# A 16-row write from SBUF to the output as SyncE's first transfer, in an RMSNorm-SiLU kernel

## The chip, the cores and the metric

The kernel runs on one core of a Trainium2 chip. A core has a matrix engine (TensorE, PE in the profile), a vector engine (VectorE, DVE), a scalar engine (ScalarE, ACT), GpSimd (POOL) and SyncE (SP), which here only issues transfers. Transfers between the memory of the chip (HBM) and the core's own memory (SBUF, 128 partitions) run on 16 DMA engines that all issuing queues share. The metric is the device time of one execution in microseconds; smaller is better.

## The reference

```python
def reference(x, gamma, eps):                 # x: 8 x 1024 x 2048 f32, gamma: 2048 f32
    rms = np.sqrt(np.mean(x ** 2, axis=-1, keepdims=True) + eps)
    out = gamma * x / rms
    return (out * (1 / (1 + np.exp(-out)))).astype(np.float32)
```

Each of the 8192 rows of 2048 numbers is divided by its root mean square, multiplied by gamma, and put through SiLU. 67.1 MB are read and 67.1 MB are written.

## The kernel before

The 8192 rows are cut into 16 blocks of 512 rows. A block lies on the 128 partitions with four rows (J = 4) on each, so a block is 4.19 MB and a partition's share of it is one contiguous run of 32 KB in HBM (blocks 4 and 5 are loaded together, with 64 KB for each partition). A ring in SBUF, `xt` (line 57), holds six blocks (BUFS = 6); a block is loaded into its place in the ring, changed in place and stored from there, so block b + 6 can be loaded only when block b has been stored.

For each block the steps are:

- `load` (line 68; line 72 for the pair of blocks 4 and 5), issued from ScalarE's queue;
- the sum of squares of each row, two of four rows on ScalarE (`squares_scalar`, line 89) and two on VectorE (`squares_vector`, line 98);
- the root on ScalarE (`root`, line 108) and its reciprocal on VectorE (`invert`, line 114);
- the product of row, reciprocal and gamma on VectorE (`multiply`, line 124);
- SiLU on ScalarE, two rows at a time (`silu`, line 129);
- `store` (line 133), issued from SyncE's queue. SyncE issues nothing else but one transfer of gamma at the start.

The order of all this is written out by hand (`tc.manual_schedule()`, line 135); every engine runs its instructions in that order and waits on semaphores where it needs another's result. Blocks 0 and 1 are done singly, the others in pairs that share one root and one reciprocal.

At the start, gamma has to be brought to all 128 partitions. SyncE loads it into the first partition of the tile `g` (line 141). TensorE multiplies it with one partition of the tile `ones` (line 144; `ones` is 128 x 128 and is filled by VectorE in line 138), VectorE copies the result from PSUM to `g` (line 146), and a one-element copy on ScalarE (line 147) waits for that. Behind this copy on ScalarE stand the loads of blocks 2 to 5; the loads of blocks 0 and 1 stand ahead of it.

```python
load(0)
nc.vector.memset(ones, 1.0)
nc.vector.memset(eps_t, float(eps))
nc.scalar.activation(out=junk_a[:, 0:1], in_=ones[:, 0:1], func=ACT.Square)
nc.sync.dma_start(out=g[0:1, :], in_=bass.AP(tensor=gamma.tensor, offset=gamma.offset, ap=[[d, 1], [1, d]]))
```

Of the kernel before, what the change touches and what calls it, by code (L numbers as in the profile page):

```python
# [1 line left out]

# [4 lines left out]

ACT = mybir.ActivationFunctionType
ALU = mybir.AluOpType


@with_exitstack
def kernel(
    ctx: ExitStack,
    tc: tile.TileContext,
    x: bass.AP,
    gamma: bass.AP,
    eps: bass.AP,
    out: bass.AP,
):  # L20

    nc = tc.nc
    P = nc.NUM_PARTITIONS
    f32 = mybir.dt.float32
    x2 = x.flatten_outer_dims()
    o2 = out.flatten_outer_dims()  # L30
    n, d = x2.shape
    J = 4
    BUFS = 6
    SINGLE = 2
    nblk = n // (P * J)
    PAIRS = (4,)

    def view(t, b):

        for q in PAIRS:  # L40
            if b in (q, q + 1):
                both = t[q * P * J:(q + 2) * P * J, :].rearrange("(p j) d -> p (j d)", p=P, j=2 * J)
                return both[:, (b - q) * J * d:(b - q + 1) * J * d]
        return t[b * P * J:(b + 1) * P * J, :].rearrange("(p j) d -> p (j d)", p=P, j=J)

    singles = ctx.enter_context(tc.tile_pool(name="singles", bufs=1))
    small = ctx.enter_context(tc.tile_pool(name="small", bufs=2))
    psum = ctx.enter_context(tc.tile_pool(name="psum", bufs=1, space=bass.MemoryType.PSUM))

    Q = 4  # L50
    w = d // Q
    g = singles.tile([P, d], f32)
    eps_t = singles.tile([P, 1], f32)
    ones = singles.tile([P, P], f32)
    junk_a = psum.tile([P, d], f32, name="junk_a")
    junk_v = psum.tile([P, d], f32, name="junk_v")
    ring = singles.tile([P, BUFS * J * d], f32, name="xt")
    sss, rmss, rstds = {}, {}, {}

    def rows(b, j, k):  # L60
        at = (b % BUFS) * J + j
        return ring[:, at * d:(at + k) * d]

    def row(b, j):
        return rows(b, j, 1)

    def load(b):
        nc.scalar.dma_start(out=rows(b, 0, J), in_=view(x2, b))  # L68

    def load_pair(b):  # L70
        both = x2[b * P * J:(b + 2) * P * J, :].rearrange("(p j) d -> p (j d)", p=P, j=2 * J)
        nc.scalar.dma_start(out=rows(b, 0, 2 * J), in_=both)

    def group(b):

        return [b] if b < SINGLE else [b, b + 1]

    def sums(b):
        if b not in sss:
            k = len(group(b))  # L80
            t = small.tile([P, k * J], f32, name="ss")
            for i, m in enumerate(group(b)):
                sss[m] = (t, i * J)
        return sss[b]

    def squares_scalar(b, loads=()):
        t, at = sums(b)
        for j in range(share(b)):
            nc.scalar.activation(out=junk_a, in_=row(b, j), func=ACT.Square,  # L89
                                 accum_out=t[:, at + j:at + j + 1])  # L90
            if j == 0:
                for s in loads:
                    load(s)

    def squares_vector(b):
        t, at = sums(b)
        for j in range(share(b), J):
            nc.vector.tensor_tensor_reduce(  # L98
                out=junk_v, in0=row(b, j), in1=row(b, j), scale=1.0, scalar=0.0,
                op0=ALU.mult, op1=ALU.add, accum_out=t[:, at + j:at + j + 1])  # L100

    def share(b):
        return 2

    def root(b):
        k = len(group(b)) * J
        rms = small.tile([P, k], f32, name="rms")
        nc.scalar.activation(out=rms, in_=sss[b][0], func=ACT.Sqrt, scale=1.0 / d, bias=eps_t)  # L108
        rmss[b] = rms

    def invert(b):
        k = len(group(b)) * J
        rstd = small.tile([P, k], f32, name="rstd")
        nc.vector.reciprocal(out=rstd, in_=rmss.pop(b))  # L114
        for i, m in enumerate(group(b)):
            rstds[m] = (rstd, i * J)

    def scale(b, j):
        t, at = rstds[b]
        return t[:, at + j:at + j + 1]  # L120

    def multiply(b):
        for j in range(J):
            nc.vector.scalar_tensor_tensor(out=row(b, j), in0=row(b, j), scalar=scale(b, j),  # L124
                                           in1=g, op0=ALU.mult, op1=ALU.mult)

    def silu(b):
        for h in range(0, J, 2):
            nc.scalar.activation(out=rows(b, h, 2), in_=rows(b, h, 2), func=ACT.Silu)  # L129
        store(b)  # L130

    def store(b):
        nc.sync.dma_start(out=view(o2, b), in_=rows(b, 0, J))

    with tc.manual_schedule():

        load(0)
        nc.vector.memset(ones, 1.0)  # L138
        nc.vector.memset(eps_t, float(eps))  # L139
        nc.scalar.activation(out=junk_a[:, 0:1], in_=ones[:, 0:1], func=ACT.Square)  # L140
        nc.sync.dma_start(out=g[0:1, :], in_=bass.AP(tensor=gamma.tensor, offset=gamma.offset, ap=[[d, 1], [1, d]]))
        for c in range(Q):
            cols = slice(c * w, (c + 1) * w)
            nc.tensor.matmul(junk_v[:, cols], ones[0:1, :], g[0:1, cols], start=True, stop=True)  # L144
        load(1)
        nc.vector.tensor_copy(out=g, in_=junk_v)  # L146
        nc.scalar.copy(out=junk_a[:, 0:1], in_=junk_v[:, d - 1:d])  # L147
        for b in range(2, PAIRS[0]):
            load(b)
        for b in PAIRS:  # L150
            load_pair(b)


        squares_scalar(0)
        squares_vector(0)
        root(0)
        invert(0)
        multiply(0)
        squares_scalar(1)
        silu(0)  # L160
        squares_vector(1)
        root(1)
        invert(1)
        multiply(1)
        squares_scalar(2)
        silu(1)
        squares_vector(2)

        for b in range(SINGLE, nblk, 2):
            squares_scalar(b + 1, [b + 3] if BUFS <= b + 1 and b + 3 < nblk else [])
            squares_vector(b + 1)
            root(b)
            invert(b)
            multiply(b)
            multiply(b + 1)
            silu(b)
            ahead = b + 2
            if ahead < nblk:  # L180
                if b == SINGLE:
                    load(BUFS)
                    silu(b + 1)
                    squares_scalar(ahead, [BUFS + 1])
                    squares_vector(ahead)
                    continue
                squares_scalar(ahead, [ahead + 2] if ahead + 2 < nblk else [])
                squares_vector(ahead)
            silu(b + 1)


# [1 line left out]
_INS = ['x', 'gamma', 'eps']  # L193
_OUTS = [((8, 1024, 2048), 'float32')]

_NUMBERS = {'eps': 9.999999747378752e-06}


# [26 lines left out]
```

## Time and profile before

| | |
|---|---|
| time, median of 3 runs | 316.79 us (316.77 to 316.83) |
| time of the profiled execution | 316.85 us |
| span of the profiled execution | 315.1 us |
| moved | 134.24 MB, 426 GB/s over the span |
| VectorE busy | 224.6 us (71%) |
| ScalarE busy | 204.6 us (65%) |
| TensorE busy | 7.2 us (2%) |
| DMA's share of the chain that ended last | 51% |
| a store, from issue to landing (median) | 41.0 us |
| a load, from issue to landing (median) | 25.4 us |

The span runs from the first to the last instruction that the profiler saw; the rest of the execution's time, 1.75 us, lies around it. In the profile q10 is the queue of the loads (ScalarE's) and q1 that of gamma and of the stores (SyncE's). "SPq" and "ACTq" are the issuing parts of SyncE and ScalarE. In the timeline a line has the start, the length, the engine, the line of the kernel, the operation, and in brackets how long the engine had been idle and what ended it; instructions of one kind that lie close together are merged, with their count behind an x.

### The profile page before, as it was taken

What the parts mean: (1) busy time and instruction counts of PE and PEld (TensorE: products, weight loads), DVE (VectorE), ACT (ScalarE), POOL (GpSimd) and SP (SyncE); (2) the same over time, 40 slices, a digit from 0 to 9 for tenths busy, and PEclk for the clock granted to TensorE, in tenths of its full rate; (3) what the DMA queues carried; (4) which work ended last, traced back from release to release, by engine and by line L of the source; (5) the groups of instructions that cost most, each with busy time, mean ns of one, the idle gap of its engine ahead of it and who ended that gap; (6) DMA issues with size and microseconds to landing.
All of it is one profiled execution on the core that took longest, in us unless ns stands there. A gap on an engine that the chain in (4) does not pass through costs nothing.

```text
span 315.1 us, 402 instructions
## 1 busy us (share of the span) xinstructions
PE 7.2 (2%) x8; PEld 2.5 (1%) x8; DVE 224.6 (71%) x140; ACT 204.6 (65%) x126; POOL 0.2 (0%) x4
## 2 busy tenths in 40 slices
PE   6200000000000000000000000000000000000000
PEld 2000000000000000000000000000000000000000
DVE  0679599799806998299923999149991599979500
ACT  1259998488365896658916689066890679957800
POOL 0000000000000000000000000000000000000000
DMA  8999999999999999999999999999999999999996
GB/s 334 412 453 412 387 528 399 399 408 458 405 458 409 453 412 453 416 449 416 449 416 449 420 445 424 441 424 441 433 433 437 433 433 433 433 433 433 437 437 300
DMA packets 4468, 134.24 MB, mean 426 GB/s; under 512 B 497, under 2 KB 497, under 8 KB 497
## 3 DMA queue, kind: packets, MB, share of 16 engines
q10 hardware_dynamic: 2160, 67.11, 49.8%
q1 hardware_dynamic: 2306, 67.12, 49.4%
q14 instruction: 2, 0.02, 0.0%
HBM read 67.12 MB, written 67.11 MB: 426 GB/s over the span
## 4 chain that ended last, share of the span: by engine, by line
DMA 51%; DVE 22%; ACT 18%; issue 3%; DVEq 1%; ACTq 0%
DMA out_dram<-xt 44%; DVE xt L124 20%; ACT xt L129 10%; DMA xt<-in_x_dram 7%; ACT junk_a L89 5%; DVE junk_v L98 2%; ACT L108 2%; DVEq L220 1%; ACT rms L108 0%; ACTq L68 0%; ACT L129 0%; DVE rstd L114 0%; DVE ss L98 0%; ACT L140 0%; ACTq L108 0%
## 5 line engine op out<-in xcount | busy, mean ns | idle before, releaser
L124 DVE SCALAR_TENSOR_TENSOR xt<-xt,rstd,g 128x2048 f32<-128x2048 f32 x64 | 145.6, 2345 | 0.3
L129 ACT ACTIVATE xt<-xt 128x4096 f32<-128x4096 f32 x32 | 115.0, 3611 | 35.9 <-DVE xt L124 35.9
L89 ACT ACTIVATE junk_a<-xt 128x2048 f32<-128x2048 f32 x32 | 59.9, 1873 | 45.8 <-DMA out_dram<-xt 41.2
L98 DVE CUSTOM_DVE_ANT_0 junk_v<-xt 128x2048 f32<-128x2048 f32 x32 | 73.5, 2298 | 1.5 <-DMA xt<-in_x_dram 0.7
L114 DVE RECIPROCAL rstd<-rms 128x8 f32<-128x8 f32 (+1 forms) x9 | 1.8, 198 | 59.8 <-ACT rms L108 59.8
L108 ACT ACT_TABLE_LOAD x9 | 11.5, 1283 | 2.1 <-DVE ss L98 1.9
L129 ACT ACT_TABLE_LOAD x9 | 11.5, 1283 | 0.2
L146 DVE COPY g<-junk_v 128x2048 f32<-128x2048 f32 x1 | 2.3, 2291 | 9.1 <-PE junk_v L144 9.1
L144 PE MATMUL junk_v<-g,ones 1*128 1x512 f32 x8 | 7.2, 1072 | 2.9 <-DMA g<-in_gamma_dram 2.9
L147 ACT COPY junk_a<-junk_v 128x1 f32<-128x1 f32 x1 | 0.1, 144 | 9.9 <-DVE g L146 9.9
L89 ACT ACTIVATION_READ_ACCUMULATOR junk_a<-xt 128x1 f32 x32 | 6.0, 186 | 0.0
L98 DVE DVE_READ_ACCUMULATOR2_ANT ss<- 128x1 f32 x32 | 4.5, 140 | 0.0
L108 ACT ACTIVATE rms<-ss,eps_t 128x8 f32<-128x8 f32 (+1 forms) x9 | 2.7, 300 | 0.1
L144 PEld LDWEIGHTS junk_v<-g,ones 1*128 1x128 f32 x8 | 2.5, 325 | 6.0 <-issue 6.0
L140 ACT ACT_TABLE_LOAD x1 | 1.3, 1283 | 1.1 <-PEq L206 1.1
L138 DVE MEMSET ones<- 128x128 f32 x1 | 0.2, 165 | 0.8 <-PEq L206 0.8
L140 ACT ACTIVATE junk_a<-ones 128x1 f32<-128x1 f32 x1 | 0.2, 174 | 0.0
L206 POOL MEMSET const-bfloat16-1.0<- 128x1 bf16 x1 | 0.1, 102 | 0.0
L206 POOL MEMSET const-uint8-127<- 128x1 uint8 x1 | 0.1, 102 | 0.0
L206 POOL MEMSET const-float32-0.0<- 128x1 f32 x1 | 0.1, 99 | 0.2 <-issue 0.2
L206 POOL MEMSET const-float32-1.0<- 128x1 f32 x1 | 0.1, 99 | 0.0
L139 DVE MEMSET eps_t<- 128x1 f32 x1 | 0.1, 59 | 0.0
## 6 DMA issues: line engine op xcount, KB each, us to landing
out_dram<-xt SPq DMA_DIRECT2D x16, 4096.0 KB, 41.0
xt<-in_x_dram ACTq DMA_DIRECT2D x14, 4096.0 KB, 25.4
g<-in_gamma_dram SPq DMA_DIRECT2D x1, 8.0 KB
xt<-in_x_dram ACTq DMA_DIRECT2D x1, 62.0
```

The lines of the kernel that those rows point to most:

```text
L89: nc.scalar.activation(out=junk_a, in_=row(b, j), func=ACT.Square, accum_out=t[:, at + j:at + j + 1])
L98: nc.vector.tensor_tensor_reduce(out=junk_v, in0=row(b, j), in1=row(b, j), scale=1.0, scalar=0.0, op0=ALU.mult, op1=ALU.add, accum_out=t[: ...
L108: nc.scalar.activation(out=rms, in_=sss[b][0], func=ACT.Sqrt, scale=1.0 / d, bias=eps_t)
L114: nc.vector.reciprocal(out=rstd, in_=rmss.pop(b))
L124: nc.vector.scalar_tensor_tensor(out=row(b, j), in0=row(b, j), scalar=scale(b, j), in1=g, op0=ALU.mult, op1=ALU.mult)
L129: nc.scalar.activation(out=rows(b, h, 2), in_=rows(b, h, 2), func=ACT.Silu)
L138: nc.vector.memset(ones, 1.0)
L140: nc.scalar.activation(out=junk_a[:, 0:1], in_=ones[:, 0:1], func=ACT.Square)
L144: nc.tensor.matmul(junk_v[:, cols], ones[0:1, :], g[0:1, cols], start=True, stop=True)
L146: nc.vector.tensor_copy(out=g, in_=junk_v)
L206: nc = _bacc.Bacc("TRN2", target_bir_lowering=False, num_devices=1)
L220: with _tile.TileContext(nc) as tc:
```

## The change

A new function, `first_words_out`, is called between ScalarE's first activation and the load of gamma. It issues one transfer from SyncE. Its source is the tile `ones`: the first 128 numbers (512 bytes) of every eighth partition, sixteen rows in all. Its destination is the place of block 15 in the output: the first 512 bytes of every eighth partition's run of 32 KB, so the sixteen pieces lie 256 KB apart. The last store of the kernel writes the whole of block 15 later, over these pieces.

```diff
     def store(b):
         nc.sync.dma_start(out=view(o2, b), in_=rows(b, 0, J))
 
+    def first_words_out():
+
+        w0, G = 128, 16
+        last = view(o2, nblk - 1).rearrange("(a c) f -> a c f", a=G)
+        nc.sync.dma_start(out=last[:, 0, 0:w0], in_=ones.rearrange("(a c) f -> a c f", a=G)[:, 0, 0:w0])
+
     with tc.manual_schedule():
 
         load(0)
         nc.vector.memset(ones, 1.0)
         nc.vector.memset(eps_t, float(eps))
         nc.scalar.activation(out=junk_a[:, 0:1], in_=ones[:, 0:1], func=ACT.Square)
+        first_words_out()
         nc.sync.dma_start(out=g[0:1, :], in_=bass.AP(tensor=gamma.tensor, offset=gamma.offset, ap=[[d, 1], [1, d]]))
```

The order of the instructions on TensorE, VectorE, ScalarE and GpSimd stays as it was; SyncE has one transfer more, ahead of gamma's. The transfers take their semaphores from eight in turn, so from gamma on each has the next one of the eight; load 6 waits for store 0, as before, and now also for the new transfer, whose semaphore it takes over.

## The prediction

> **What bounds the kernel now.** I read the page first, for the DMA rows. Columns of the two slice rows: forty slices of 7.9 us; the first row is the mean busy share of the 16 DMA engines in tenths, the second what they moved.
>
> ```profile
> span 315.1 us, 402 instructions
> DMA  8999999999999999999999999999999999999996
> GB/s 334 412 453 412 387 528 399 399 408 458 405 458 409 453 412 453 416 449 416 449 416 449 420 445 424 441 424 441 433 433 437 433 433 433 433 433 433 437 437 300
> DMA packets 4468, 134.24 MB, mean 426 GB/s; under 512 B 497, under 2 KB 497, under 8 KB 497
> q10 hardware_dynamic: 2160, 67.11, 49.8%
> q1 hardware_dynamic: 2306, 67.12, 49.4%
> ```
>
> The transfers never rest: all slices but the first and last are at nine tenths or more, and the rate without mixing (late slices) is 433 GB/s, 27.06 GB/s for one of 16 engines. 134.24 MB at 433 take 310.0 us of the span of 315.1. VectorE (71%) and ScalarE (65%) have room. So only two things can change the time: packet time that carries no bytes, and a moment with nothing queued.
>
> For the first I set the DMA share of some stretches beside the bytes of the same stretches (columns: stretch, length, busy of five engines with counts, clock, DMA share, GB/s).
>
> ```profile
> 1.00:4.00 3.00, 1.09 (x2) 0.60 (x3) 0.00 (x0) 1.46 (x2) 0.00 (x0) 1.00 0.96 319
> 4.00:20.00 16.00, 6.07 (x8) 1.89 (x6) 7.38 (x7) 5.73 (x7) 0.00 (x0) 1.00 1.00 432
> 36.00:40.00 4.00, 0.00 (x0) 0.00 (x0) 3.18 (x3) 3.96 (x5) 0.00 (x0) 1.00 1.10 385
> 40.00:52.00 12.00, 0.00 (x0) 0.00 (x0) 11.93 (x8) 11.38 (x8) 0.00 (x0) 1.00 1.01 437
> 52.00:68.00 16.00, 0.00 (x0) 0.00 (x0) 14.23 (x10) 9.50 (x7) 0.00 (x0) 1.00 1.06 459
> ```
>
> A share of 1.00 goes with 432 to 433 GB/s: in 4 to 20, in 40 to 52 (437 by 1.01) and in 52 to 68 (459 by 1.06). Two stretches break this. In 36 to 40 the engines are booked 1.10 x 4 = 4.40 us each, and the bytes need 385/432.5 x 4 = 3.56: on the mean engine 0.84 us of packet time without bytes. In 1 to 4 it is 2.88 against 2.21: 0.67 us. The second is load 0, the first reads of x. What is the first?
>
> ```profile
> 0.72 0.38 ACTq L68 DMA_DIRECT2D xt<-in_x_dram  x1
> 0.73 0.33 SPq L141 DMA_DIRECT2D g<-in_gamma_dram  x1
> 0.82 0.17 DVE L138 MEMSET ones<- 128x128 f32 x1 [0.82 <-PEq L206]
> 2.91 7.16 PE L144 MATMUL junk_v<-g,ones 1*128 1x512 f32 x8 [2.91 <-DMA g<-in_gamma_dram]
> 12.51 0.82 ACTq L68 DMA_DIRECT2D xt<-in_x_dram  x2
> 22.67 1.88 ACT L89 ACTIVATE junk_a<-xt 128x2048 f32<-128x2048 f32 x1 [3.11 <-DMA xt<-in_x_dram]
> 28.86 2.29 DVE L98 CUSTOM_DVE_ANT_0 junk_v<-xt 128x2048 f32<-128x2048 f32 x1
> 35.17 35.51 SPq L133 DMA_DIRECT2D out_dram<-xt  x3
> ```
>
> The timeline has one event ahead of it: SyncE issues the first store at 35.17, the first transfer of the kernel from SBUF to HBM. Later stores begin without such a loss. The single packet records, strung by their times into the 16 engines, say the same finer: every engine loses 0.47 to 1.59 us on the load packets between 36 and 40, mean 0.84, and the engine that ends last in the whole kernel is the one that lost 1.59. Taking from each engine its own loss brings the last end forward by 0.82 us (the next engines lost 0.75 and 0.90).
>
> **The change, part by part.** It removes nothing and adds one transfer, which I call the touch: from SBUF to the output, sixteen rows of 512 B, on SyncE ahead of gamma. No engine's compute instructions change, and loads and stores keep their order.
>
> *The touch's bytes.* One row for each engine, if it is split as loads are: 512/27,060 = 0.02 us, and a count for the semaphore. The packet price has no row of its own. Bounds: nothing below; above, the whole time in which engines are booked or waiting beyond the bytes, 315.1 - 310.0 = 5.1 us, less the two losses (1.5), shared over 497/16 = 31 small packets an engine: 0.12 us each, 0.23 for two. The small-packet row bounds it loosely, since start and end of the span are in it; I take 0.08.
>
> *The touch's wait.* It reads the tile of ones, so it waits for the memset, 0.82 + 0.17 = 0.99. Behind it on SyncE is gamma alone, which went out at 0.73 and now follows at about 1.0 + 0.41 (two loads took 0.82) = 1.4: 0.7 late. On its DMA engine gamma also meets load 0, which it used to precede: up to one load packet more (32 KB at 27.06 GB/s = 1.21), and up to another around the touch. So gamma comes 0.7 to 3.1 late, and I take 1.9.
>
> The Trainium skill, DMA: Bandwidth & Descriptors, section "Queues, rings and completion order", says that a DMA engine takes turns between the queues it has work for, one packet at a time. By that rule gamma's delay would be the 1.9, not the 0.7.
>
> *Who waits for gamma.* The matmuls (7.16), the copy of g, ScalarE's copy at 12.49, behind which loads 2 to 5 stand, then block 0's work. Loads 0 and 1 keep the DMA engines busy to 22.65, and a load takes about 1 us from issue to its first packet (0.72 to the 1 to 2 us stretch), so loads 2 to 5 may be some 9 us late. Block 0: ScalarE ends root 0 at 19.56 and waits 3.11 until 22.67 for block 1; the second silu starts near 31.6 and its rows are done at 28.86, 2.7 earlier; VectorE's squares of block 1 end at 33.6 and ScalarE wants them at 35.16, 1.5 later. A delay of 1.9 costs store 0 nothing and root 1 about 0.4; and at 36 the DMA engines still have 24 MB less 34 us x 433 GB/s = 10 MB of loads queued, 23 us of work. It costs nothing. Were that cover gone, it would cost up to 3.1.
>
> *New waits later.* The queues' semaphores move on by one place: load 6 also waits for the touch, and the last store lies over bytes that the touch wrote. Load 6 is issued at 67.41, some 60 us after the touch. The tail holds too: the last store, issued at 299.7, lands 13.9 later, where its 4.19 MB need 9.7 and its start 1, so about 3 us of older stores cover any lateness.
>
> *The first-store loss.* If it belongs to the first write from SBUF to the output, whichever it is, the touch takes it, at about 2 to 3 us instead of 36 to 40. There load 0's own empty 0.67 us runs. Not shown by the trace: how much of the touch's stall lies under it. Bounds: all of it (the end comes 0.82 sooner, 0.08 for the touch: -0.74) and none (0.84 paid at the start: about +0.10). That gamma's engine ran gamma before load 0 and still lost time at store 0 says that the loss is not a matter of SyncE's queue being new. I take the full cover as likeliest: gamma's first read and load 0's first reads were in flight together, and gamma landed (matmul at 2.91) before load 0's empty time was over, so first accesses overlap there. Sum: 315.1 - 0.82 + 0.08 = 314.4 span; the profiled execution took 316.85 with 1.75 around its span, and the median is 316.79, so **316.05**, 0.23% faster. 0.2% (0.63 us) is about what a measurement of this kernel can tell from no change.
>
> **Rivals.**
> *The loss is moved, not hidden.* The touch stalls load 0's packets at the start as store 0 stalls load packets now. For it: at store 0 the packets that lost time are loads, on another queue. Against: load 0 is waiting anyway. Time 316.79 + 0.08 - up to 0.4 of partial cover: 316.4 to 316.9, middle 316.7.
> The Trainium skill, DMA: Bandwidth & Descriptors, section "Back-pressure in remote DMA", states that stalled writes hold up the other queues of the same engine. It speaks of transfers between cores; by it this rival would hold and the time would be 316.7. The trace agrees that loads are held when store 0 begins; whether they would be at 2 us no run shows yet.
>
> *The loss belongs to a queue that starts beside a running one.* After the touch the queue is empty until 35.17, so store 0 loses its 0.84 again, and the touch adds its packets: 316.85. For it: the queue of stores is never empty again until the end, so no restart shows it free. In this case the change has no hold on the loss at all.
>
> *Slower: both are paid.* The loss belongs to the part of the output that is first written. The touch writes in block 15's place, 15 x 4.19 = 63 MB behind block 0's; it stalls all engines at the start (0.84) and store 0 stalls them again. 316.79 + 0.84 + 0.08 = 317.7. It decides if stores 0 to 15 each had such a loss; against it, the stretches after 40 us show none, though each store goes to a new 4 MB.
>
> **Chances and range.** Hidden at least in the main 0.50, moved 0.20, restart 0.14, both paid 0.16. The first's own range is 315.7 (some engines' lateness gone too) to 316.3, with 0.42 of its 0.50 beyond 0.63 us. Faster 0.42; same 0.08 + 0.20 + 0.14 = 0.42; slower 0.16. The range for 8 in 10 leaves out most of the last: 315.75 to 317.1.
>
> **What would show it.** DMA share and bytes of the stretch 36 to 40 should agree again (1.00 by 432); if 1.10 by 385 stays, the restart or the both-paid case holds. In 1 to 4 the difference should stay near 0.67; if it grows to 1.5, the loss was moved. Gamma's matmul should begin at 3.6 to 6 instead of 2.91, store 0 be issued at 35.2 to 35.7, and the last landing come 0.7 sooner. I am wrong if an idle DMA stretch appears anywhere after 4 us, or if the last store is issued over 3 us later against the bytes left.

## The result, and the profile after

The changed kernel took 319.40 us (median of four, 319.28 to 320.12), the kernel before 316.81 in the same comparison: a ratio of 1.0087, 95% interval 1.0075 to 1.0098. The change costs 2.6 us. Forecast were 316.05 and a range of 315.75 to 317.1.

The rows of the page that answer to those shown of the kernel before (the profiled execution took 320.12 us, the longest of the four, so what follows explains 3.2 us and not 2.6):

```profile
span 318.3 us, 404 instructions
DMA  8999999999999999999999999999999999999995
GB/s 330 409 449 432 424 395 453 420 399 399 432 409 417 445 441 420 445 416 441 428 441 445 416 445 424 432 436 432 449 412 445 424 436 436 432 441 420 441 424 235
DMA packets 4500, 134.25 MB, mean 422 GB/s; under 512 B 513, under 2 KB 529, under 8 KB 529
```

The transfers still never rest. There are 32 packets more: sixteen of the touch and sixteen counts of its semaphore. So the time has gone where no row of tenths shows it. The timeline of the changed kernel:

```profile
0.72 0.37 ACTq L68 DMA_DIRECT2D xt<-in_x_dram  x1
1.02 0.58 SPq L139 DMA_DIRECT2D out_dram<-ones  x1
1.66 0.45 SPq L148 DMA_DIRECT2D g<-in_gamma_dram  x1
10.61 7.16 PE L151 MATMUL junk_v<-g,ones 1*128 1x512 f32 x8 [10.61 <-DMA g<-in_gamma_dram]
20.21 0.82 ACTq L68 DMA_DIRECT2D xt<-in_x_dram  x2
40.32 16.05 SPq L133 DMA_DIRECT2D out_dram<-xt  x2
72.99 0.33 ACTq L68 DMA_DIRECT2D xt<-in_x_dram  x1
76.57 0.33 SPq L133 DMA_DIRECT2D out_dram<-xt  x1
```

Gamma goes out 0.93 us later than before (1.66 against 0.73) and lands 7.7 us later: its matmul starts at 10.61, not 2.91. The loads of blocks 2 to 5 follow at 20.21 (12.51 before), store 0 at 40.32 (35.17), load 6 at 72.99. In the kernel before load 6 went out 5.6 us earlier:

```profile
67.41 0.34 ACTq L68 DMA_DIRECT2D xt<-in_x_dram  x1
```

The stretches, read as in the prediction (DMA share times length, less the time that the bytes need at 432.5 GB/s):

```profile
1.00:4.00 3.00, 0.00 (x0) 0.00 (x0) 0.00 (x0) 1.46 (x2) 0.00 (x0) 1.00 0.99 317
36.00:40.00 4.00, 0.00 (x0) 0.00 (x0) 3.97 (x4) 3.44 (x2) 0.00 (x0) 1.00 0.91 393
40.00:52.00 12.00, 0.00 (x0) 0.00 (x0) 10.26 (x7) 10.68 (x9) 0.00 (x0) 1.00 1.04 410
52.00:68.00 16.00, 0.00 (x0) 0.00 (x0) 14.15 (x12) 10.38 (x8) 0.00 (x0) 1.00 1.01 432
68.00:100.00 32.00, 0.00 (x0) 0.00 (x0) 25.61 (x17) 25.23 (x15) 0.00 (x0) 1.00 1.00 414
100.00:200.00 100.00, 0.00 (x0) 0.00 (x0) 79.55 (x49) 70.07 (x40) 0.00 (x0) 1.00 1.00 432
```

The loss of 36 to 40 us has only moved with store 0: it is now in 40 to 52 (12.48 - 11.38 = 1.10 us on the mean engine), and 52 to 68 has 0.18. New is 68 to 100: 32.00 - 30.63 = 1.37 us of packet time without bytes, where the kernel before had none (30.40 - 30.41):

```profile
68.00:100.00 32.00, 0.00 (x0) 0.00 (x0) 19.79 (x15) 20.32 (x14) 0.00 (x0) 1.00 0.95 411
```

In all 2.65 against 0.84, so 1.8 us more on the mean engine. In 1 to 4 us little changed: 2.97 - 2.20 = 0.77, against 0.67. The packet records, strung into the 16 engines as in the prediction, give the rest: the engines end 1.83 us later on average, and the last of them 2.0 us behind the mean instead of 0.6. 1.83 + 1.40 = 3.2, the difference of the spans, 318.3 - 315.1.

The packet records also tell why gamma is so late. Times in us from the start of the span, rounded; the touch's and gamma's packets are on SyncE's queue:

```
                          before            changed kernel
first load packets        1.7 to 2.5        1.7 to 2.3
touch, 16 packets         -                 6.1 to 6.6
touch, 16 counts          -                 7.3 to 7.9
gamma's packet            1.7               8.6
gamma's count             2.5              10.1
```

On every engine three load packets run ahead of the touch. Then each packet of SyncE's queue waits for one load packet of 1.21 us, and a four-byte count is a packet too: touch, load, count, load, gamma, load, count.

### The profile page after: what moved, and what is told of

The parts are those of the page before. It is cut to its first block, busy times and chain, and to the rows that moved or that the text cites. A ratio compares the mean times of both kernels' runs of the same rounds, so it can differ in the third digit from the quotient of the medians.

```text
span 318.3 us, 404 instructions
## 1 busy us (share of the span) xinstructions
PE 7.2 (2%) x8; PEld 2.5 (1%) x8; DVE 224.6 (71%) x140; ACT 205.0 (64%) x126; POOL 0.2 (0%) x4
## 4 chain that ended last, share of the span: by engine, by line
DMA 54%; DVE 26%; ACT 10%; PE 2%; issue 2%; DVEq 1%; ACTq 1%; SPq 0%
DMA out_dram<-xt 42%; DVE xt L124 19%; DMA xt<-in_x_dram 9%; ACT xt L129 6%; DVE junk_v L98 5%; DMA g<-in_gamma_dram 3%; PE junk_v L151 2%; ACT L108 2%; ACT junk_a L89 2%; DVE g L153 1%; DVEq L227 1%; ACT rms L108 0%; ACTq L68 0%; DVE rstd L114 0%; DVE ss L98 0%
```

## Experiments

Two theories stood at first. *Late gamma*: the touch costs only because gamma lands late, and with it block 0's work. *The touch itself*: sixteen rows on the store queue, or an early write to the output, make later transfers dearer.

**The touch behind gamma.**

```diff
-        first_words_out()
         nc.sync.dma_start(out=g[0:1, :], in_=...)
+        first_words_out()
```

> Gamma's load and the touch change places on SyncE; both stay. Theory of the late gamma (the touch costs only because gamma now lands at 10.6 us instead of 2.9, and store 0 goes out at 40.3 instead of 35.2): gamma's matmul near 2.9 us, store 0 near 35.2, time 316.5 to 317.1. Theory of the touch itself (sixteen rows on the store queue make the later stores dearer, whenever gamma comes): 318.5 to 319.5 with matmul near 2.9. If besides the touch takes over the loss of the first store, the stretch 36 to 40 agrees with its bytes and the time is 316.0.

Measured: 316.83 us against 316.71, ratio 0.9998 (0.9989 to 1.0007). Lines of its timeline and three of its stretches:

```profile
1.14 0.56 SPq L139 DMA_DIRECT2D out_dram<-ones  x1
2.57 7.16 PE L151 MATMUL junk_v<-g,ones 1*128 1x512 f32 x8 [2.57 <-DMA g<-in_gamma_dram]
35.24 0.37 SPq L133 DMA_DIRECT2D out_dram<-xt  x1
```

```profile
1.00:4.00 3.00, 1.43 (x2) 0.83 (x3) 0.00 (x0) 1.46 (x2) 0.00 (x0) 1.00 0.93 319
36.00:40.00 4.00, 0.00 (x0) 0.00 (x0) 3.11 (x3) 3.96 (x5) 0.00 (x0) 1.00 1.07 352
68.00:100.00 32.00, 0.00 (x0) 0.00 (x0) 19.39 (x14) 20.38 (x14) 0.00 (x0) 1.00 0.96 414
```

The same touch is there, and the whole cost is gone; 68 to 100 loses 30.72 - 30.63 = 0.1 us. The theory of the touch itself falls. And the first-store loss is still there: 4.28 - 3.26 = 1.02 us in 36 to 40 (0.84 before), while 1 to 4 loses 2.79 - 2.21 = 0.58 (0.67 before). The touch takes over nothing.

**Gamma late without a touch.** Gamma's transfer waits for two clearings of its row by VectorE:

```diff
+        for _ in range(2):
+            nc.vector.memset(g[0:1, :], 0.0)
         nc.sync.dma_start(out=g[0:1, :], in_=...)
```

> No touch; gamma's transfer waits for two clearings of its own row by VectorE and so lands several us late. Late gamma: matmul at 7 to 11 us, store 0 at 37 to 41 us, time 318 to 319.5. Touch itself: 316.8.

Measured: 320.93 us (320.57 to 321.65), ratio 1.0130 (1.0112 to 1.0147). It was later than meant, hence above the 319.5:

```profile
5.40 0.33 SPq L143 DMA_DIRECT2D g<-in_gamma_dram  x1
11.83 2.04 PE L146 MATMUL junk_v<-g,ones 1*128 1x512 f32 x2 [11.83 <-DMA g<-in_gamma_dram]
41.54 0.36 SPq L133 DMA_DIRECT2D out_dram<-xt  x1
```

Late gamma alone slows the kernel. Issued at 5.40, it still takes 6.4 us to its matmul, with nothing of SyncE's ahead of it. Here loads 2 to 5, issued at 21.43, also came too late: by the packet records the mean engine stands idle for 0.7 us before 30 us, against none in the kernel before. That is likely why this run costs more than the changed kernel.

**A read in the touch's place**, of the same shape, from x into a spare tile:

```diff
-        last = view(o2, nblk - 1)...
-        nc.sync.dma_start(out=last[:, 0, 0:w0], in_=ones...)
+        last = view(x2, nblk - 1)...
+        nc.sync.dma_start(out=spare...[:, 0, 0:w0], in_=last[:, 0, 0:w0])
```

> The touch is replaced by a transfer of the same shape and place in the queue that reads sixteen 512-byte rows of x into a spare tile; nothing is written to the output ahead of store 0. Late gamma: as the changed kernel, matmul near 10.6 and 319.2 to 319.6. A cost of writing the output early: under 318.

Measured: 319.70 us, ratio 1.0085 (1.0071 to 1.0100), matmul at 10.58. VectorE clears the spare tile first (not shown in the cut of the edit), so the read goes out at 1.16, the touch at 1.02. Whether the sixteen rows are written to the output or read from x makes no difference that these runs show.

**Loads 2 to 5 ahead of the copy that waits for gamma**, in the changed kernel:

```diff
+        for b in range(2, PAIRS[0]): load(b)
+        for b in PAIRS: load_pair(b)
         nc.vector.tensor_copy(out=g, in_=junk_v)
         nc.scalar.copy(out=junk_a[:, 0:1], in_=junk_v[:, d - 1:d])
-        for b in range(2, PAIRS[0]): load(b)
-        for b in PAIRS: load_pair(b)
```

> The changed kernel, with the loads of blocks 2 to 5 issued ahead of ScalarE's copy that waits for gamma. Gamma stays late. If the lateness of these loads costs, about 317; if the lateness of block 0's work and of store 0 costs, 319 to 319.6, with store 0 still after 39 us.

Measured: 319.09 us, ratio 1.0073 (1.0058 to 1.0089), store 0 at 40.03. The lateness of these loads is at most 0.3 of the 2.6 us; block 0's late work carries the rest.

**Gamma behind a small clearing, no touch.**

```diff
+        nc.vector.memset(g[0:1, 0:128], 0.0)
         nc.sync.dma_start(out=g[0:1, :], in_=...)
```

> No touch; gamma's transfer waits only for a small clearing by VectorE, so it goes out at about 1.2 us, 0.5 later than before but behind load 0. If being behind load 0's packets is the larger part of gamma's delay (three load packets of 1.21 us ahead, one more before its count): matmul at 7.5 to 8.5 us, store 0 near 37.5 to 39. Time: half of the late gamma's cost, 317.3 to 318.8. If gamma is only 0.5 late: matmul near 3.5 and 316.8.

Measured: 317.81 us, ratio 1.0038 (1.0017 to 1.0060); the ten runs lie in two groups of five, 316.8 to 317.2 and 318.4 to 319.4, and the median lies between them. The profiled run, 318.43, is of the upper group.

```profile
1.15 0.33 SPq L142 DMA_DIRECT2D g<-in_gamma_dram  x1
8.30 5.45 PE L145 MATMUL junk_v<-g,ones 1*128 1x512 f32 x6 [8.30 <-DMA g<-in_gamma_dram]
38.01 0.37 SPq L133 DMA_DIRECT2D out_dram<-xt  x1
```

```profile
68.00:100.00 32.00, 0.00 (x0) 0.00 (x0) 23.60 (x17) 23.32 (x15) 0.00 (x0) 1.00 0.96 395
```

Gamma goes out 0.42 us later and lands 5.4 us later. That is the price of losing the place ahead of load 0's packets; the other 2.3 of the changed kernel's 7.7 are the touch's packet and its count. With store 0 at 38.01 this run loses 30.72 - 29.23 = 1.49 us in 68 to 100. No run of the lower group was traced; that a store 0 near 38 us lies on the edge where the cost begins is a guess.

**What the lateness does downstream.** In the changed kernel the packet records show the queue of loads empty from 69 to 71 us (the end of blocks 4 and 5) until load 6 begins at 77.5 to 79.9, a gap of 8.5 to 8.7 us on every engine; the longest gap before was 2.4. Load 6 needs block 0's place, and store 0 ends at 71.4 to 72.3. It also stands on ScalarE behind block 2's second SiLU, which starts at 72.93 (66.70 before) and here comes last. Blocks 4 and 5 come in packets of 64 KB, so beside store 0's 32 KB the loads get two thirds of an engine. New theory, *the empty load queue*: it is this that loses the time of 68 to 100.

Load 6 late in the kernel before:

```diff
-                    load(BUFS)
                     silu(b + 1)
+                    load(BUFS)
```

> The kernel before, with load 6 moved on ScalarE behind the SiLU of block 3, from 67.4 to about 76 us; gamma, store 0 and all work of blocks 0 to 3 stay where they were. Theory of the empty load queue (what the late gamma costs is that the queue of loads runs dry near 70 us and starts again with load 6 near 78): packet time without bytes between 72 and 92 us rises from 0.03 to 0.8 or more on the mean engine, time 317.8 to 320. Theory that only the late start of store 0 and of block 0's work costs: 316.8.

Measured: 321.05 us (median of ten, 317.30 to 322.06), ratio 1.0108 (1.0076 to 1.0141), but not in the way expected. Two stretches of the profiled run, at 318.77 one of the faster, and one of the kernel before:

```profile
72.00:100.00 28.00, 0.00 (x0) 0.00 (x0) 20.13 (x15) 19.44 (x14) 0.00 (x0) 1.00 0.95 411
290.00:300.00 10.00, 0.00 (x0) 0.00 (x0) 10.00 (x5) 8.01 (x3) 0.00 (x0) 1.00 0.86 370
```

```profile
290.00:300.00 10.00, 0.00 (x0) 0.00 (x0) 6.07 (x3) 7.91 (x3) 0.00 (x0) 1.00 1.04 449
```

With a gap of 6.0 us in the loads no packet time is lost (26.60 booked, 26.61 needed). The cost lies at the end, where 290 to 300 moves 370 GB/s instead of 449: the last loads are late, and stores run short. That an empty load queue loses packet time each time is refuted. The runs above 320 us were not traced.

Equal packets: blocks 4 and 5 as two single blocks, in the changed kernel and, second, in the kernel before (the edit is the same in both):

```diff
-    PAIRS = (4,)
+    PAIRS = ()
-        for b in range(2, PAIRS[0]):
+        for b in range(2, BUFS):
             load(b)
-        for b in PAIRS:
-            load_pair(b)
```

> The changed kernel with blocks 4 and 5 loaded one by one, with 32 KB for each partition. Empty load queue: packets of 64 KB gave the loads two thirds of the engines while store 0 ran; with equal packets store 0 is over sooner and the loads last longer, so load 6 comes in time and the loss of 72 to 92 us is under 0.3; time at most 1 us above the next kernel. Otherwise: 2 to 3 us above it.

> The kernel before with blocks 4 and 5 loaded one by one: the base for the kernel above. Both theories: 316.5 to 318.

Measured: with the touch 317.17 us (316.85 to 319.47), ratio to the kernel before 1.0038 (1.0012 to 1.0064); without it 322.28 us, 1.0174 (1.0158 to 1.0189). The first agrees, with 0.05 us lost in 72 to 92 by the packet records of the profiled run (317.10), though three of its eight runs took 318.9 to 319.5; the second missed by over 4 us. To part packet size from the rows' layout, the same with the layout kept:

```diff
         for b in PAIRS:
-            load_pair(b)
+            load(b)
+            load(b + 1)
```

> The changed kernel with blocks 4 and 5 loaded by two transfers, the rows in memory as in the kernel before: packets of 32 KB instead of 64. Gamma is as late as with the touch. Empty load queue: with equal packets the loads last until load 6 starts, no gap over 3 us between loads, loss of 72 to 92 us under 0.2 on the mean engine, time 316.9 to 317.5. If the loss hangs on the late block 0 itself: 319 and more.

> The kernel before with the same two transfers: base of the kernel above. With gamma early, store 0 and load 6 come early against the longer loads, and the last loads come late: the tail runs empty, 321 to 323, 5 to 6 us idle after 290 us. If the row layout was what made the kernel with single loads slow: 316.8.

Measured: with the touch 317.18 us (316.89 to 320.76), ratio 1.0026 (0.9999 to 1.0052), longest gap in the loads 2.8 us (two of the ten runs, 319.47 and 320.76, stand apart and were not traced):

```profile
40.00:52.00 12.00, 0.00 (x0) 0.00 (x0) 10.26 (x7) 10.84 (x9) 0.00 (x0) 1.00 1.02 412
68.00:100.00 32.00, 0.00 (x0) 0.00 (x0) 28.02 (x18) 25.24 (x15) 0.00 (x0) 1.00 0.99 427
```

Matmul at 10.71 and store 0 at 40.93, as late as in the changed kernel, yet 68 to 100 loses 31.68 - 31.59 = 0.1 instead of 1.37. Load 6 goes out at 73.60, no earlier than in the changed kernel, but the loads before it now last until 78.8. Without the touch 322.25 us, ratio 1.0170 (1.0153 to 1.0187):

```profile
290.00:300.00 10.00, 0.00 (x0) 0.00 (x0) 10.00 (x6) 7.47 (x3) 0.00 (x0) 1.00 0.49 210
```

Here the DMA engines stand half idle at the end. So the packet size decides, not the layout: with 64 KB packets the kernel runs well with early gamma and badly with late gamma, with 32 KB packets the other way round. In none of these is a version that beats the kernel before.

**Store 0 in halves**, in the kernel before, each half behind its SiLU:

```diff
+            if b == 0:
+                nc.sync.dma_start(out=view(o2, b)[:, h * d:(h + 2) * d], in_=rows(b, h, 2))
-        store(b)
+        if b > 0:
+            store(b)
```

> The kernel before with store 0 in two transfers of 16 KB rows, each behind its half of SiLU, so the first goes out at 31.6 us. If the loss of the first store belongs to any first long store beside running loads: 0.6 to 1.0 us lost just after 33 us, none at the second, 316.6 to 317.0. If it grows with the row's length: under 0.5, time 316.3 to 316.6.

Measured: 318.17 us, ratio 1.0038 (1.0023 to 1.0053), slower than either theory said.

```profile
20.00:36.00 16.00, 0.00 (x0) 0.00 (x0) 13.35 (x8) 13.41 (x8) 0.00 (x0) 1.00 0.98 408
36.00:40.00 4.00, 0.00 (x0) 0.00 (x0) 3.34 (x3) 3.96 (x5) 0.00 (x0) 1.00 0.97 414
68.00:100.00 32.00, 0.00 (x0) 0.00 (x0) 20.90 (x15) 20.15 (x14) 0.00 (x0) 1.00 0.98 418
```

The first half pays the loss (15.68 - 15.09 = 0.59, its issue is at 31.51), the second almost none (0.05). And packets of 16 KB beside 64 KB let store 0 end so late that load 6 goes out at 71.60, the loads have a gap of 6.7 to 8.5 us, and 68 to 100 loses 0.43: a smaller loss in the same place, reached with gamma early.

**Load 6 late in the changed kernel**, the edit of the sixth experiment, to see whether the loss needs load 6 to start ahead of store 2:

> The changed kernel with load 6 moved behind the SiLU of block 3, so that store 2 (76.6 us) goes out before load 6 (82 to 86) instead of 3.6 us after it; the load queue is empty for longer. If the loss of packet time at 72 to 92 us needs only a load queue that ran empty: still 0.6 or more on the mean engine after 72 us. If it needs load 6 to start while store 1 alone is left, ahead of store 2: under 0.3. The time itself says nothing on this, since late loads empty the tail (318 to 325).

Measured: 325.80 us, one run, with 316.97 for the kernel before beside it.

```profile
68.00:100.00 32.00, 0.00 (x0) 0.00 (x0) 28.02 (x18) 25.23 (x15) 0.00 (x0) 1.00 0.99 408
```

Load 6 is issued at 82.14, after store 2, the gap is over 16 us, and 31.68 - 30.19 = 1.49 us are lost. The order of the two is not what it takes.

What these runs settle: the slowdown is gamma's lateness. It makes the work of the first blocks late, and with it store 0 and load 6; in the changed kernel, where 64 KB packets let the loads run out early, packet time is then lost in 68 to 100.

What stays open is why it is lost. The length of the gap does not decide it. By the packet records, strung into engines, nine engines of the changed kernel start load 6 at 77.5 to 77.8 after gaps of 8.5 us and lose under 0.1 there. The other seven start it at 79.4 to 79.9 after gaps of 8.5 to 8.7, lose 1.3 to 1.5 each, nearly all in one store packet just ahead of load 6's first, and are the seven that end last (315.9 to 317.1, the nine at 314.1 to 314.6). The run of gamma behind a small clearing has gaps of 4.8 to 9.2 and loses 1.49 on the mean engine; load 6 late in the kernel before lost none after 6.0. The other half of the loss comes some 10 us later on every engine, 0.5 to 0.9, in load packets within 3 us of the end of store 1 and the start of store 2. As at store 0, the time is lost on one queue about where a transfer of the other begins; but from 100 us on transfers begin without such a loss (0.2 us on the mean engine in 100 us), and no run here isolates the cause.

## Why the prediction was wrong, point by point

**Bound: right.** The DMA engines bound the kernel, and only packet time without bytes could change it. All of the 3.2 us of the profiled span came that way; no idle stretch appeared.

**Gamma's delay: the step that failed.** It was put at 0.7 to 3.1 us, taken as 1.9, and measured 7.7. The issue time was nearly right (1.4 forecast, 1.66 measured). What was wrong is the count of load packets: one to two, where six run ahead of gamma's count. Three run before the first SyncE packet, and one comes after each packet of SyncE's, where counts are packets too. The profile before could have told the first part: store 0, issued at 35.17, has its first packet at 39.5 to 41.7 in the packet records, three load packets later. The Trainium skill's rule, DMA: Bandwidth & Descriptors, section "Queues, rings and completion order", of turns taken packet by packet was applied to data alone; the trace agrees with it, one packet of 1.21 us for each turn, once the counts are included.

**Who waits for gamma: the slacks were right, the conclusion fell with the delay.** The slack was given as 2.7 us at the second SiLU; 7.7 less that is 5.0, and store 0 went out 5.15 later. "It costs nothing" rested on queued loads that keep the engines busy. They did, but busy was not enough: what the delay cost was packet time without bytes, some 30 to 50 us later, when the loads ran out ahead of load 6. "Up to 3.1" without cover was about the size seen, 2.6, by another route; that closeness is chance.

**The first-store loss: wrong.** The touch neither hid it nor moved it to the start; with gamma early (first experiment) it stayed at 1.02. The rival of the queue that starts beside a running one described this part, and gave 316.85 for it; that experiment measured 316.83. The rule behind the rival of the moved loss (the Trainium skill, DMA: Bandwidth & Descriptors, section "Back-pressure in remote DMA") is not seen at work in these sixteen 512-byte writes: between 5 and 20 us, where they run in that experiment, the mean engine loses 0.04 us by the packet records, against 0.03 without them.

**The slower rival: right in sign, wrong in kind.** "Both are paid" gave 317.7 from a stall at the start that did not come (0.77 us in 1 to 4, 0.67 before). No rival priced a gamma that comes 5 us after its slack has run out, though the views for it were on the table: the wait for gamma was dismissed by the bound of 3.1.

## What to carry to other kernels

A small transfer on the critical chain of the start is worth its place ahead of the bulk transfers, not only on its own queue: 0.42 us of later issue cost gamma 5.4 us of landing, since three bulk packets ran first and one more came between any two packets of its queue. When something is put ahead of such a transfer, count packets, counts of semaphores included, each with one bulk packet. And a kernel whose DMA engines are always busy still has a balance between its queues: the packet sizes beside each other, and with them the order in which buffers come free, moved this one by up to 5.5 us with the same bytes (316.7 against 322.3).

## What the runs showed of the hardware that was not expected

- A semaphore's count waits its turn like data: the touch's 512 bytes take 0.027 us on an engine, and its count follows 1.23 us later, behind a load packet.
- The first long store beside running loads costs the mean engine 0.6 to 1.2 us in the load packets around its first packets, whatever small transfer went before (0.84 in the kernel before, 1.02 with the touch behind gamma, 1.10 in the changed kernel).
- Two queues share an engine by packets, not by bytes: 64 KB packets beside 32 KB ones had two thirds of it, and store 0 needed eight turns of 3.6 us.
- In the changed kernel the lost time is not spread evenly, and the last engine sets the time: the mean engine ends 1.83 us later than before, the last one 3.2, and the seven engines that lost 1.3 to 1.5 us at load 6's start are the last seven.
